# Recurrent gates as three passes of split operands in a hybrid decoder trunk

## The chip, the cores and the metric

The kernel runs on one core of one Trainium2 chip. The metric is the device time of one execution in microseconds, here the median of three runs. Engines are named as the profile names them: PE is TensorE (PEld its weight loads), DVE is VectorE, ACT is ScalarE, POOL is GpSimd, SP is SyncE, which issues the large transfers.

## The reference

A trunk of two layers on 256 tokens of width 2048. Each layer norms its input, projects it to all branches at once, runs three branches (a gated causal convolution, a recurrent block, sparse attention), weighs their outputs with sigmoid gates and projects the sum; a squared-ReLU MLP of width 8192 follows. The part that the change touches is the recurrent block (RG-LRU) on 768 channels, six blocks of 128:

```
def rg_lru(x, wa, ba, wx, bx, lam):
    xb = x.reshape(b, s, RNN_BLOCKS, RNN_BLOCK_W)
    r = sigmoid(einsum('bsnc,ncd->bsnd', xb, wa).reshape(b, s, d) + ba)
    i = sigmoid(einsum('bsnc,ncd->bsnd', xb, wx).reshape(b, s, d) + bx)
    log_a = -RG_C * softplus(-lam) * r
    a = exp(log_a)
    gated_x = sqrt(-expm1(2.0 * log_a)) * (i * x)
    _, h = associative_scan(_lin_combine, (a, gated_x), axis=1)
...
    r = causal_depthwise_conv(r_x, rnn_conv_w[l], rnn_conv_b[l])
    r = rg_lru(r, ...)
    p_b = (r * gelu(r_gate)) @ w_rnn_out[l]
```

All arrays are float32. `x` here is the block's convolved input, and `wa`, `wx` are six 128x128 matrices each, one per block and gate.

## The kernel before

Activations lie with channels on the 128 partitions and the 256 tokens (S) along the free dimension. All large matrices are streamed from HBM in tiles of up to 128x1024: SP fetches a tile `raw`, ACT copies it to `wh`, rounded to float32r (`wpart`, lines 192 to 196), and DVE subtracts to get the rest, `wl`. Activations are split in the same way by `split` (line 208) into two halves of one tile of the pool `hl` (34 tiles). A product of one 128x128 block (`tile2`, line 217) is then two instructions: `wh` times both halves (512 columns) and `wl` times the first half (256 columns), both in float32r. `wnext` keeps three weight tiles ahead (AHEAD), and the pool holds four.

The units of a layer follow the list PLAN (line 68): 38 units of the branches' inputs, then the 16 output-gate units "ga" with the 16 units "pa" of the convolution's output projection set between them from the seventh on, then "gb" with "pb" (recurrent branch), then "gc" with "pc" (attention), each in the same pattern, with the short units of the compression's matrices among "ga". A "pc" unit multiplies six blocks of `oh`, three per group of heads. A gate unit has 16 blocks. The layer ends with the output projection and the MLP.

Beside this stream run side tasks, as Python generators in the list `side`: `conv_task`, `rnn_task` and `attn_task`, strictly one after the other. Each step up to a `yield` is issued by `pump` (line 272) between weight tiles. `pump` works with a planner's clock per engine (`clk`): each helper (`tt`, `stt`, `ts`, `act`, `mm`, lines 132 to 157) adds a fixed charge for its instruction, what a side step charges on DVE and ACT counts 1.4 times (SLACK), and a step is issued only while the clocks of DVE and ACT are behind that of PE. So these charges decide where in the program a side task's steps stand. Ahead of the first unit that needs a task's result, `finish` (line 784) issues whatever steps are left of it.

From this program order a scheduler (line 1023) makes the order on each engine, by its own estimate of times; it may take a later instruction ahead where an earlier one's operands are not ready by that estimate. `keep` fixes the order of single instructions.

`rnn_task` (line 415) takes the six blocks `m` in turn: the two gates' matrices of the block come by a DMA that POOL issues (`ruw`, 128x256), the four-tap convolution makes `rc` on DVE, two plain float32 products (lines 423 and 424) make both gates in one PSUM tile, and Tanh, Exp and Sqrt on ACT, DVE arithmetic and a scan make the block's output, which is split into `rb_` tiles for "pb".

Of the kernel before, what the change touches and what calls it, by code (L numbers as in the profile page):

```python
# [10 lines left out]
F32R = mybir.dt.float32r  # L11
# [7 lines left out]
S = 256  # L19
# [74 lines left out]
def trunk(ctx: ExitStack, tc: tile.TileContext, a, out):  # L94
# [15 lines left out]
    def hl(dt=F32, name="hl"):  # L110
        return hlp.tile([128, 2, S], dt, tag="hl", name=name)

    def tmp(name="t"):
        return tp.tile([128, S], F32, tag="t", name=name)
# [4 lines left out]
    def big_ps():  # L119
        return psu.tile([128, 512], F32, tag="u", name="pu")  # L120

    def side_ps():
        return pss.tile([128, 512], F32, tag="s", name="pv")

    def fsz(ap):
        n = 1
        for s in ap.shape[1:]:
            n *= s
        return n


    def tt(o, x, y, op):
        clk["v"] += 0.07 + fsz(o) / 960
        return V.tensor_tensor(o, x, y, op=op)  # L134

    def stt(o, x, s, y, op0, op1):
        clk["v"] += 0.07 + fsz(o) / 960
        return V.scalar_tensor_tensor(o, x, s, y, op0=op0, op1=op1)  # L138

    def ts(o, x, s1, s2, op0, op1=None):  # L140
        clk["v"] += 0.07 + fsz(o) / 1920
        if op1 is None:
            return V.tensor_scalar(o, x, s1, None, op0=op0)
        return V.tensor_scalar(o, x, s1, s2, op0=op0, op1=op1)

    def act(o, x, f, bias=None, scale=1.0, accum=None):
        clk["act"] += 0.2 + fsz(o) / 1200
        kw = {}
        if bias is not None:
            kw["bias"] = bias  # L150
        if accum is not None:
            kw["accum_out"] = accum
        return A.activation(o, x, f, scale=scale, **kw)  # L153

    def mm(o, l, r, start, stop, passes=1):
        clk["pe"] += (passes * max(64, fsz(r)) if passes > 1 else max(256, fsz(r))) / 2400 + 0.002
        return T.matmul(o, l, r, start=start, stop=stop)  # L157

    def f32(ap):
        return ap.bitcast(F32)  # L160
# [47 lines left out]
    def split(dst, src, scale=None):  # L208

        if scale is None:  # L210
            act(dst[:, 0, :], src, AF.Copy)
            tt(dst[:, 1, :], src, f32(dst[:, 0, :]), ALU.subtract)
        else:
            act(dst[:, 0, :], src, AF.Copy, scale=scale)
            stt(dst[:, 1, :], src, scale, f32(dst[:, 0, :]), ALU.mult, ALU.subtract)
# [154 lines left out]
    def causal_conv(o, u, w, b, k):  # L370

        ts(o, u, w[:, k - 1:k], b, ALU.mult, ALU.add)
        yield
        for d in range(1, k):
            stt(o[:, d:], u[:, :S - d], w[:, k - 1 - d:k - d], o[:, d:], ALU.mult, ALU.add)
            yield
# [38 lines left out]
    def rnn_task(l, rx, gg, rb_out):  # L415
        rw = par[:, l, P_RW:P_RW + 24]
        for m in range(6):
            rc = tmp("rconv")
            ruw = tmp("ruw")
            keep(G.dma_start(ruw, a["rgw"][l, m]))  # L420
            yield from causal_conv(rc, rx[m], rw[:, 4 * m:4 * m + 4], par[:, l, P_RB + m:P_RB + m + 1], 4)
            p = side_ps()
            mm(p[:, :S], ruw[:, :128], rc, True, True, 4)
            mm(p[:, S:], ruw[:, 128:], rc, True, True, 4)
            tr, ti, t2 = tmp("tr"), tmp("ti"), tmp("t2")
            act(tr, p[:, :S], AF.Tanh, bias=hpar[:, l, 132 + m:133 + m], scale=0.5)
            act(ti, p[:, S:], AF.Tanh, bias=hpar[:, l, 138 + m:139 + m], scale=0.5)
            s2, s4 = sp2[:, l, m:m + 1], sp4[:, l, m:m + 1]

            act(t2, tr, AF.Tanh, bias=s2, scale=s2)  # L430
            act(tr, tr, AF.Exp, bias=s4, scale=s4)
            yield
            stt(t2, tr, 1.0, t2, ALU.add, ALU.mult)
            ts(tr, t2, -1.0, 1.0, ALU.mult, ALU.add)
            stt(t2, t2, 2.0, t2, ALU.subtract, ALU.mult)
            act(t2, t2, AF.Sqrt, scale=-0.25)
            yield
            stt(ti, ti, 1.0, rc, ALU.add, ALU.mult)
            tt(ti, ti, t2, ALU.mult)
            h = rc  # L440
            clk["v"] += 0.6
            V.tensor_tensor_scan(h, tr, ti, 0.0, op0=ALU.mult, op1=ALU.add)
            yield
            tt(h, h, gg[m], ALU.mult)
            r = hl(F32R, "rb_")
            split(r, h, 0.5)
            rb_out.append(r)
            yield
# [255 lines left out]
    for l in range(L):  # L704

        rc, rb = None, None
# [22 lines left out]
        def evict(nm, m, z):  # L729
# [16 lines left out]
            elif nm == "rgate":  # L746
# [5 lines left out]
                if m == 5:  # L752
                    rt = rnn_task(l, rx, gg, rbt)
                    side.append(rt)
# [26 lines left out]
        for ui, (nm, m) in enumerate(PLAN):  # L781
# [7 lines left out]
            if l == 0 and ui < 2:  # L789
                p = early[ui]  # L790
            else:
                p = big_ps()
# [22 lines left out]
        for m in range(KT):  # L815
            p = big_ps()
# [214 lines left out]
```

## Time and profile before

| | us |
|---|---|
| median of three runs | 2850.17 |
| lowest and highest | 2849.88 and 2850.19 |
| the profiled execution | 2849.82 |
| its span, first to last instruction | 2848.1 |

| engine | busy us | share of the span |
|---|---|---|
| PE | 2836.5 | 100% |
| PEld | 2490.8 | 87% |
| DVE | 2095.5 | 74% |
| ACT | 1473.7 | 52% |
| POOL | 91.1 | 3% |

A profile of one execution lists each instruction with its start and length from the span's start. A record's length includes the time in which the engine's pipeline drains, so consecutive records on PE overlap; what an instruction costs there is read from the distance of the starts. A group's line gives the count, then busy time and mean length, then the idle time before it and what ended that. PE's granted clock is full (0.999 on average).

### The profile page before, as it was taken

To read this page: it belongs to the slowest core of one execution; us is meant where nothing else is said; L and a number is where in the kernel's file an instruction comes from. 1 tells how busy PE (TensorE), PEld (TensorE's weight loads), DVE (VectorE), ACT (ScalarE), POOL (GpSimd) and SP (SyncE) were. 2 spreads that over 40 slices of the span, in tenths; PEclk is the share of its full clock that TensorE was granted. 3 is DMA by queue.
4 is the path that set the end of the run, shared out by engine and by line. 5 is a ranking of instruction groups with operands and counts; after the bars stand their busy time and mean duration, and the time that the engine had idled before them with its cause. 6 is when DMAs were issued, how large, how long until landed. Compare 5 with 4: busy or idle time off the path is not lost.

```text
span 2848.1 us, 43089 instructions
## 1 busy us (share of the span) xinstructions
PE 2836.5 (100%) x16420; PEld 2490.8 (87%) x16420; DVE 2095.5 (74%) x3388; ACT 1473.7 (52%) x2253; POOL 91.1 (3%) x88
## 2 busy tenths in 40 slices
PE   9999999999999999999999999999999999999998
PEld 7888888888888888888888888888888888888887
DVE  7988888777676676666779888786777766766655
ACT  6547765555444443443545587555554444434444
POOL 0000000002000000000200000000020000000001
PEclk9999999999999999999999999999999999999999
DMA  7555655465556555555555556545655555555554
GB/s 241 191 189 175 218 173 162 164 194 192 189 189 191 190 189 191 191 189 191 191 187 190 185 187 215 160 159 178 196 188 189 189 191 189 190 191 190 191 191 148
DMA packets 153454, 534.28 MB, mean 188 GB/s; under 512 B 17312, under 2 KB 18208, under 8 KB 153248
## 3 DMA queue, kind: packets, MB, share of 16 engines
q1 hardware_dynamic: 152192, 529.15, 56.6%
q8 instruction: 128, 2.10, 0.3%
q0 software_dynamic: 768, 2.13, 0.3%
q14 instruction: 78, 0.64, 0.1%
q10 hardware_dynamic: 288, 0.26, 0.0%
HBM read 529.37 MB, written 2.10 MB: 187 GB/s over the span
## 4 chain that ended last, share of the span: by engine, by line
PE 99%; DMA 0%; DVE 0%; ACT 0%; SPq 0%; issue 0%; POOLq 0%; DVEq 0%; ACTq 0%
PE pu L157 96%; PE pv L157 3%; PE pv L658 0%; DMA x<-in_xT_dram 0%; DMA raw<-in_win_dram 0%; DVE fin L134 0%; ACT wh L153 0%; PE pv L616 0%; DVE wl L134 0%; PE pv L526 0%; ACT xhl L153 0%; SPq L194 0%; SPq L688 0%; POOLq L1023 0%; DVE sq L134 0%
## 5 line engine op out<-in xcount | busy, mean ns | idle before, releaser
L153 ACT ACTIVATE wh<-raw 128x1024 fp32r<-128x1024 f32 (+2 forms) x1036 | 1067.9, 1031 | 1293.3 <-PE pu L157 682.1
L157 PE MATMUL pu<-xhl,wh 128*128 128x512 f32 x4800 | 1678.1, 393 | 0.9 <-DVE xhl L138 0.5
L134 DVE TENSOR_TENSOR wl<-raw,wh 128x1024 fp32r<-128x1024 f32 (+2 forms) x1036 | 1229.3, 1187 | 597.7 <-ACT wh L153 577.6
L157 PE MATMUL pu<-xhl,wl 128*128 128x256 f32 x4800 | 1346.3, 281 | 0.4 <-DVE wl L134 0.2
L157 PEld LDWEIGHTS pu<-xhl,wh 128*128 128x128 f32 x4800 | 898.2, 187 | 199.2 <-ACT wh L153 1.9
L157 PEld LDWEIGHTS pu<-xhl,wl 128*128 128x128 f32 x4800 | 906.8, 189 | 3.9 <-DVE wl L134 1.2
L157 PE MATMUL pu<-ah,wh 128*128 128x512 f32 x2016 | 699.1, 391 | 0.0
L157 PE MATMUL pu<-ah,wl 128*128 128x256 f32 x2016 | 564.5, 280 | 0.0
L157 PEld LDWEIGHTS pu<-ah,wh 128*128 128x128 f32 x2016 | 377.0, 187 | 82.7
L157 PEld LDWEIGHTS pu<-ah,wl 128*128 128x128 f32 x2016 | 381.0, 189 | 0.0
L134 DVE TENSOR_TENSOR x<-x,pu 128x256 f32<-128x256 f32 x316 | 132.8, 421 | 87.8 <-PE pu L157 82.6
L157 PE MATMUL pu<-yhl,wh 128*128 128x512 f32 x512 | 177.5, 393 | 0.0
L331 POOL TENSOR_TENSOR ssq<-ssq,sq 128x256 f32<-128x256 f32 x55 | 73.8, 1342 | 2175.3 <-ACT sq L153 2170.7
L157 PE MATMUL pu<-yhl,wl 128*128 128x256 f32 x512 | 141.7, 277 | 0.0
L157 PEld LDWEIGHTS pu<-yhl,wh 128*128 128x128 f32 x512 | 95.8, 187 | 22.0
L134 DVE TENSOR_TENSOR z<-pu,z 128x256 f32<-128x256 f32 x268 | 111.5, 417 | 0.8 <-ACT z L153 0.8
L138 DVE SCALAR_TENSOR_TENSOR cacc<-u,hpar,cacc 128x255 f32<-128x255 f32 (+14 forms) x240 | 103.5, 462 | 0.0
L153 ACT ACTIVATE z<-pu 128x256 f32<-128x256 f32 x268 | 98.2, 367 | 1.2 <-PE pu L157 1.2
L157 PEld LDWEIGHTS pu<-yhl,wl 128*128 128x128 f32 x512 | 96.2, 188 | 0.2
L157 PE MATMUL pu<-oh,wh 128*128 128x512 f32 x192 | 67.4, 391 | 0.0
L134 DVE TENSOR_TENSOR z<-z,rb 128x256 f32<-128x256 f32 x136 | 57.4, 424 | 4.3
L138 DVE SCALAR_TENSOR_TENSOR s<-z 128x256 f32<-128x256 f32 x128 | 54.1, 424 | 4.3
(295 smaller groups left out, 1702.7 us busy)
## 6 DMA issues: line engine op xcount, KB each, us to landing
raw<-in_win_dram SPq DMA_DIRECT2D x340, 512.0 KB, 3.3
raw<-in_wup_dram SPq DMA_DIRECT2D x256, 512.0 KB, 4.3
raw<-in_wdn_dram SPq DMA_DIRECT2D x256, 512.0 KB, 4.3
raw<-in_wo_dram SPq DMA_DIRECT2D x64, 512.0 KB, 3.3
raw<-in_wro_dram SPq DMA_DIRECT2D x32, 384.0 KB, 3.1
raw<-in_wao_dram SPq DMA_DIRECT2D x32, 384.0 KB, 3.1
raw<-in_wco_dram SPq DMA_DIRECT2D x32, 256.0 KB, 3.1
raw<-in_cw_dram SPq DMA_DIRECT2D x16, 512.0 KB, 4.6
```

What stands on the lines that cost most here:

```text
L134: return V.tensor_tensor(o, x, y, op=op)
L138: return V.scalar_tensor_tensor(o, x, s, y, op0=op0, op1=op1)
L153: return A.activation(o, x, f, scale=scale, **kw)
L157: return T.matmul(o, l, r, start=start, stop=stop)
L331: G.tensor_tensor(ssq[0], ssq[0], q, op=ALU.add)
```

## The change

In each of the six steps of `rnn_task`, the block's convolved input `rc` and its two matrices `ruw` are split into a float32r part and the rest, as the stream's operands are. Each gate is then three float32r products of 256 columns (first part by first part, first by rest, rest by first) that add up in the same PSUM half, where it was one plain float32 product. A `yield` stands between the splits and the products. The two new tiles come from the pool `hl`. In the planner's charges a block's products go from 2 x 4 x 256 to 6 x 256 columns, and two copies on ACT and two subtractions on DVE are added.

```diff
@@ rnn_task
             yield from causal_conv(rc, rx[m], rw[:, 4 * m:4 * m + 4], par[:, l, P_RB + m:P_RB + m + 1], 4)
+            rs, rws = hl(F32R, "rs"), hl(F32R, "rws")
+            split(rws, ruw)
+            split(rs, rc)
+            yield
             p = side_ps()
-            mm(p[:, :S], ruw[:, :128], rc, True, True, 4)
-            mm(p[:, S:], ruw[:, 128:], rc, True, True, 4)
+            for i in range(2):
+                o, (wh, wl) = p[:, i * S:(i + 1) * S], (rws[:, k, i * 128:(i + 1) * 128] for k in range(2))
+                mm(o, wh, rs[:, 0, :], True, False)
+                mm(o, wh, rs[:, 1, :], False, False)
+                mm(o, wl, rs[:, 0, :], False, True)
             tr, ti, t2 = tmp("tr"), tmp("ti"), tmp("t2")
```

## Rows read from the trace of the kernel before

**Rows 1.** The page: busy time by engine, and the chain that ended last.

```profile
PE 2836.5 (100%) x16420; PEld 2490.8 (87%) x16420; DVE 2095.5 (74%) x3388; ACT 1473.7 (52%) x2253; POOL 91.1 (3%) x88
...
PE 99%; DMA 0%; DVE 0%; ACT 0%; SPq 0%; issue 0%; POOLq 0%; DVEq 0%; ACTq 0%
```

**Rows 2.** Busy by stretch: length, PE, PEld, DVE, ACT, POOL; clock, DMA, GB/s.

```profile
216.00:332.00 116.00, 116.00 (x679) 101.98 (x678) 101.60 (x193) 93.24 (x155) 5.19 (x9) 1.00 0.60 197
...
1640.00:1726.00 86.00, 86.00 (x500) 75.68 (x499) 74.55 (x143) 70.12 (x114) 3.21 (x6) 1.00 0.59 195
```

**Rows 3.** Tile `ruw`: count, shortest/median/longest ns, first and last start in us.

```profile
L157 PE MATMUL pv<-rconv,ruw x48: 377/379/380, 232.9 to 1716.1; 128*128 128x256 f32 x48
```

**Rows 4.** Timeline of PE around the first block's gates: start, length in us.

```profile
232.55 0.39 PE L157 MATMUL pu<-xhl,wh 128*128 128x512 f32 x1
232.78 0.28 PE L157 MATMUL pu<-xhl,wl 128*128 128x256 f32 x1
232.90 1.03 PE L157 MATMUL pv<-rconv,ruw 128*128 128x256 f32 x4
233.57 0.58 PE L157 MATMUL pu<-xhl,wh 128*128 128x512 f32 x1
233.99 0.28 PE L157 MATMUL pu<-xhl,wl 128*128 128x256 f32 x1
```

**Rows 5.** Timeline of PE in the last unit (lines 886 to 888).

```profile
2828.42 0.40 PE L157 MATMUL pu<-wh,ah 128*128 128x256 f32 x2
2828.66 0.28 PE L157 MATMUL pu<-wl,ah 128*128 128x256 f32 x1
2828.78 0.40 PE L157 MATMUL pu<-wh,ah 128*128 128x256 f32 x2
```

**Rows 6.** Groups by line and tile: splits of 128x256 elsewhere in the kernel.

```profile
L153 ACT ACTIVATE ua<-lny 128x256 fp32r<-128x256 f32 x4 | 1.5, 406 | 0.0
L134 DVE TENSOR_TENSOR krl<-krf,krh x8: 416/418/421, 355.3 to 1762.1; 128x256 fp32r<-128x256 f32 x8
```

**Rows 7.** Timeline of DVE: one weight tile's subtraction.

```profile
283.37 1.21 DVE L134 TENSOR_TENSOR wl<-raw,wh 128x1024 fp32r<-128x1024 f32 x1
```

**Rows 8.** Timeline of PE: that tile's first use, and a later place.

```profile
285.44 0.28 PE L157 MATMUL pu<-xhl,wl 128*128 128x256 f32 x1
...
288.37 0.40 PE L157 MATMUL pu<-ua,wh 128*128 128x512 f32 x1
288.61 0.28 PE L157 MATMUL pu<-xhl,wl 128*128 128x256 f32 x1
```

**Rows 9.** The last block's output in layer 0: its reader and its writer.

```profile
L157 PE MATMUL pu<-rb__3455,wh x16: 391/396/473, 396.8 to 496.0; 128*128 128x512 f32 x16
...
L138 DVE SCALAR_TENSOR_TENSOR rb__3455<-rconv,rb__3455 x1: 419/419/419, 329.7 to 329.7; 128x256 fp32r<-128x256 f32 x1
```

**Rows 10.** Timeline of DVE: the last write of `oh` in either layer.

```profile
530.42 0.28 DVE L134 TENSOR_TENSOR oh<-pv,oh 128x128 fp32r<-128x128 f32 x1
...
1935.10 0.28 DVE L134 TENSOR_TENSOR oh<-pv,oh 128x128 fp32r<-128x128 f32 x1
```

**Rows 11.** Timeline of PE: the first product on `oh` in either layer.

```profile
541.92 0.39 PE L157 MATMUL pu<-oh,wh 128*128 128x512 f32 x1
...
1954.92 0.39 PE L157 MATMUL pu<-oh,wh 128*128 128x512 f32 x1
```

**Rows 12.** Timeline of ACT: the end of attention in layer 0.

```profile
508.29 0.46 ACT L153 ACTIVATE e<-pv,nm 128x256 f32<-128x256 f32 x1
...
515.20 1.23 ACT L153 ACTIVATE eh<-pv 128x384 fp32r<-128x384 f32 x3
...
522.09 0.49 ACT L153 ACTIVATE eh<-pv 128x384 fp32r<-128x384 f32 x1 [0.42 <-PE pv L658]
```

**Rows 13.** Busy by stretch, as rows 2: two "pc" units, then a gate unit.

```profile
541.93:546.25 4.32, 4.32 (x27) 3.83 (x26) 3.07 (x5) 2.85 (x6) 0.00 (x0) 1.00 0.57 185
546.09:551.80 5.71, 5.71 (x35) 5.05 (x34) 4.99 (x10) 2.94 (x6) 0.00 (x0) 1.00 0.73 215
```

## The prediction

> **What bounds the kernel now.** The page's first two parts and its chain of waits come first: TensorE (PE) is busy for 2836.5 of 2848.1 us, and 99% of the chain that ended last is PE, nearly all of it products of the weight stream at line 157 [rows 1]. The table by stretch shows the same where the gates run: in 216 to 332 us (layer 0) and 1640 to 1726 us (layer 1) PE is busy all the time, VectorE (DVE) for 101.60 of 116.00 and 74.55 of 86.00 us, ScalarE (ACT) for 93.24 and 70.12 [rows 2]. So a PE microsecond saved is a microsecond of the end, and work on ACT or DVE costs nothing until PE waits for it. Two things can make it wait: a weight tile that is split too late, and an activation that is ready too late. In the order of PE's instructions, I look at the gates, then at the tightest weight tile, then at the next place where PE needs what the side tasks make: the first product on `oh`, at unit "pc" 0.
>
> **What the change removes on PE.** The gates are 24 plain float32 products, 48 records, the first at 232.9 and the last at 1716.1 us [rows 3]. The PE timeline of the first channel: four records start at 232.90, the next stream product at 233.57, and that one takes 0.42 us to its successor (233.99) where an ordinary 512-column product takes 0.23 (232.55 to 232.78) [rows 4]. The channel therefore costs 233.99 - 232.90 - 0.23 = 0.86 us. The eleven others follow the same pattern. 12 x 0.86 = 10.3 us.
>
> **What it adds on PE.** Six float32r products of 128x128 by 256 columns per channel. The same form runs in the kernel's tail: from 2828.42 to 2828.78 us three start, 0.12 us each, and so on through the unit [rows 5]. Six are 0.72 us, and the slowed product behind the float32 ones goes. Per channel 0.86 - 0.72 = 0.14 us, in all 12 x 0.14 = 1.7 us. Bounds: half of an ordinary 512-column product, 0.23 / 2 = 0.115 us, would give 0.69 a channel and 2.0 in all; if the slowed product (0.42 - 0.23 = 0.19 us too long) stayed behind the new ones too, the channel would lose 0.05 and all together 0.6 us. I take 1.7, since the tail's rows have the very shape and the same three passes.
>
> The Trainium skill (FP8 and Floating Point Precision, section TensorE Precision Notes) says that true FP32 makes four passes through the array. By passes alone three in place of four would save a quarter, 12 x 0.215 = 2.6 us, against 1.7 by the rows. The trace has 0.43 us a float32 product against 0.12 for one pass, 3.6 times, so a narrow pass costs more than its share and I go by the rows.
>
> **What it adds beside PE.** Two splits per channel: on ACT two copies of 128x256 to float32r at 0.41 us, on DVE two subtractions at 0.42 us [rows 6]; 0.82 and 0.84 us a channel, 9.8 and 10.1 us in all. In layer 0's stretch 4.9 us more on ACT and 5.0 on DVE would still fit (DVE 106.6 of 116). Work that hides them: the weight stream on PE. What is queued behind them on ACT and DVE are the splits of weight tiles `wh` and `wl`, for which PE waits in the end. The tightest such tile: its subtraction starts at 283.37 and takes 1.21 us, so it ends at 284.58 [rows 7], and PE uses it at 285.44 [rows 8], a margin of 0.86 us. Worked out for each tile in the same manner, this margin is around 6 us in most of the stream; it falls to 1 to 4 in 265 to 340 and 1680 to 1770 us, where the short "pa" tiles come. One split set in front of a tile there could cost PE up to 0.84 + 0.82 - 0.86 = 0.8 us.
>
> DMAs, queues on SP and POOL, and PSUM tiles stay as they are. `ruw` is free earlier (after its split, no longer after the product). Two more tiles of the pool `hl` live for a short time per channel; by a count of what lives then (gates, values, `ua`, `rb`) some 30 of 34 are in use: no wait taken, and a short one is in the range.
>
> **What it moves.** This is the larger matter. The side tasks run one after the other (convolution, recurrent branch, attention), and `pump` (lines 272 to 279) lets a step run only when the planner's clocks of DVE and ACT are behind that of PE. By lines 132 to 157 a channel charges DVE: the convolution 0.20 + 3 x 0.33, then 0.34 + 0.20 + 0.34, then 0.34 + 0.34 + 0.60, then 0.34 + 0.34, about 4.0; the two new subtractions add 2 x 0.34 = 0.67, a sixth more. All of it counts 1.4 times (SLACK). A gate unit charges PE 16 x 0.324 = 5.18 and DVE 2 x 1.14 + 2 x 0.34 = 2.95, so it leaves 2.23 for side steps; 0.94 more per channel then needs 0.94 / 2.23 = 0.42 of a unit, 2.2 of the planner's us, 13 for six channels. During "pa" units nearly nothing is left for side steps, and each added step waits for a whole call of `pump`; carried through the plan unit by unit, the charges put the recurrent task's end 25 (layer 0) and 31 (layer 1) planner's us later (these are places in the program, not times on the chip). Its result has room: in layer 0 the last channel's is written at 329.7 and PE first takes it at 396.8 us [rows 9], and layer 1 has more. Attention starts that much later, and it has less room. By the same arithmetic its last step stood 18 and 31 planner's us ahead of "pc" 0; now it comes right at it in layer 1, and in layer 0 some steps are left over, which `finish` (line 784) places in front of "pc" 0.
>
> The trace says what that is worth. Now `oh` is complete at 530.42 + 0.28 = 530.7 and 1935.4 us [rows 10] and PE begins "pc" 0 at 541.92 and 1954.92 [rows 11]: 11.2 and 19.5 us of slack. One block of a unit takes PE 0.35 us (232.55 to 232.90 [rows 4]) where the planner charges 0.324, so a planner's us is 1.08 us: the last step is placed 19.5 and 33.6 us ahead of "pc" 0, and its result lags its place by 8.3 and 14.1 us. The chain shows why: from the last softmax exponentials at 508.29 over the four transposed groups (515.20, 522.09) to the last `oh` at 530.7 are 22 us of ACT, DVE and PE in turn [rows 12]. With the last step placed at "pc" 0, `oh` is complete some 8 to 14 us after PE arrives there. No row shows PE waiting there, so I bound it. Below: nothing, if other work fills the gap. The order is not rigid: at 288.37 one product of the next unit (`ua`) stands inside a unit on `xhl` [rows 8], so the scheduler fills PE with later work when the next is not ready. What can fill: the first half of "pc" 0 and 1, whose three blocks of `oh` are done earlier (half of their 4.32 us, 2.2), the next gate unit (5.71 us [rows 13]), the first halves of "pc" 2 and 3 (2.2), and attention's own last products: about 10 us. Above: 8.3 + 14.1 = 22 us, if nothing fills. Against 10 us of cover, 8 to 14 us leave 0 in layer 0 and up to 4 in layer 1, somewhat more if the left-over steps crowd. I take 2.5 us for both together, nearer to zero since rows 8 show the filling.
>
> **The sum.** The profiled execution took 2849.82 us, 1.7 of it outside its span; the median shown is 2850.17, 0.35 above. From the median: 2850.17 - 1.7 + 2.5 = 2851.0.
>
> **The rivals.** (1) The end of attention becomes the bound: the gap in front of "pc" 0 is not filled. For it: the lag of 8 to 14 us is measured, and layer 0's left-over steps come in one piece. Against: the filling at 288.37. It decides slower once the two stalls exceed 1.7 + 5.7 = 7.4 us. Price: half filled, 11 us, 2859.5; not filled, 22 us, 2870.5. (2) Weight tiles come late: for it the margin of 0.86 us; against, that the planner spreads the side steps when they cost more, so that DVE is no denser than now. Nine or ten tiles 0.8 us late make 7.5 us, 2856; fewer stay within the bound of no change. (3) Everything is filled and only the gates tell: 2848.5. It is the lower part of my forecast. (4) Faster than that: the gates' 10.3 us bound any gain, and six products can't be had for nothing (2.0 us by the bound above); over 0.2% would need stalls elsewhere to vanish, and the page has PE busy all along.
>
> **Chances.** A difference of 0.2% (5.7 us) is about what a measurement of this kernel can tell from no change. Stalls of 0 to 7.4 us (2848.5 to 2855.9, rival 3 within): 0.71. Rival 1: 0.21, rival 2: 0.06, together slower 0.27. Faster: 0.02. The range from 2848.0 to 2862 takes in the bounds of the gates' price and rival 1 with half its gap filled; what lies above, with little filled, is about 0.1.
>
> **What would show it.** Right: PE's busy time in the gates falls to 0.72 us a channel with starts of 0.12; the recurrent task's last channel comes some 25 to 35 us later than now (1716.1 in layer 1); the last `oh` is written within a few us of the first product on `oh`, and products on `xhl` stand between the halves of "pc" 0. Wrong: idle time of PE put down to `oh`, in front of the fourth block of "pc" 0, of over 4 us a layer (rival 1); idle time put down to `wl` in 265 to 370 or 1680 to 1800 us (rival 2); attention that ends where it does now, in which case the moved steps were mis-sized.

## The result, and the profile after

The changed kernel takes 2876.3 us (median of four executions; 2873.28 to 2877.46) against 2850.2 before: ratio 1.0089, 95% interval 1.0078 to 1.0101, so 26 us slower. The forecast was 2851.0, the range ended at 2862. The profiled execution took 2873.28 us, its span 2871.5 (2848.1 before).

The page of the changed kernel: busy time by engine, and the chain that ended last (the lines of [rows 1]).

```profile
PE 2844.7 (99%) x16444; PEld 2494.7 (87%) x16444; DVE 2099.5 (73%) x3412; ACT 1484.9 (52%) x2277; POOL 91.4 (3%) x88
...
PE 97%; DVE 1%; ACT 1%; DMA 1%; issue 0%; SPq 0%; POOLq 0%; DVEq 0%; ACTq 0%
```

PE's busy time rose by 8 us though its products became cheaper, the chain has 1% each of DVE and ACT in it where it had none, and the splits are there (24 records more on ACT and DVE each). Where PE waited, in the view of waits (us in total, times, longest):

```profile
PE pu L157 <- DVE z L134: 11.8, 7, 3.1
...
PE pu L157 <- DVE oh L134: 1.4, 2, 0.7
PE pu L157 <- ACT wh L153: 1.1, 2, 0.8
...
PE pu L157 <- DVE wl L134: 0.6, 3, 0.2
PE pv L157 <- DVE rs L134: 0.5, 1, 0.5
```

The largest line is new: in the kernel before, PE never waits for `z`. The tile `z` takes the low half of a finished unit out of PSUM (ACT), DVE adds the high half, and only then is the unit's PSUM bank free. A product that waits for `z` waits for one of four banks. Weight tiles (`wh` 1.1 and `wl` 0.6 us, against 0.4 and 0.2 before) matter little.

The stretches (length, PE, PEld, DVE, ACT, POOL; clock, DMA, GB/s) in which this happens, the first and third as in [rows 2], the other two at the attention's ends; below them the kernel before at its attention's ends:

```profile
216.00:332.00 116.00, 112.16 (x653) 98.38 (x652) 94.90 (x180) 86.91 (x150) 5.19 (x9) 0.97 0.57 187
540.00:570.00 30.00, 26.75 (x138) 22.14 (x137) 20.91 (x48) 16.27 (x41) 0.00 (x0) 0.94 0.34 107
1640.00:1726.00 86.00, 83.53 (x491) 73.42 (x490) 70.93 (x136) 66.45 (x115) 2.15 (x4) 1.00 0.52 174
1968.00:1992.00 24.00, 21.26 (x121) 17.72 (x120) 13.79 (x30) 11.93 (x25) 0.00 (x0) 1.00 0.35 114
```

```profile
540.00:570.00 30.00, 30.00 (x175) 26.43 (x174) 22.80 (x38) 17.09 (x30) 0.00 (x0) 1.00 0.58 186
1952.00:1976.00 24.00, 24.00 (x140) 21.14 (x139) 18.17 (x31) 14.12 (x24) 0.00 (x0) 1.00 0.60 185
```

PE stands for 3.8, 3.3, 2.5 and 2.7 us in them; before it was busy all the time. DVE and ACT are less busy in the gate stretches than before (94.90 against 101.60, 86.91 against 93.24 in layer 0), although the splits are added: part of the side steps now stands behind the stretch (the recurrent branch's last result comes at 368.6 us, before at 330.1), so it is not their time that runs short here.

The gate stretch of layer 0, the ACT timeline of the changed kernel (start, length; in brackets the idle time before and who ended it):

```profile
270.02 1.06 ACT L153 ACTIVATE wh<-raw 128x1024 fp32r<-128x1024 f32 x1 [0.46 <-ACT t L153]
271.24 0.42 ACT L153 ACTIVATE rb__2703<-rconv 128x256 fp32r<-128x256 f32 x1 [0.15 <-DVE rconv L134]
271.56 0.40 ACT L153 ACTIVATE rws<-ruw 128x256 fp32r<-128x256 f32 x1
271.87 0.40 ACT L153 ACTIVATE rs<-rconv 128x256 fp32r<-128x256 f32 x1
272.80 1.06 ACT L153 ACTIVATE wh<-raw 128x1024 fp32r<-128x1024 f32 x1 [0.53 <-ACT rs L153]
273.87 1.28 ACT L153 ACT_TABLE_LOAD   x1
275.17 0.47 ACT L153 ACTIVATE tr<-pv,hpar 128x256 f32<-128x256 f32 x1
275.54 0.47 ACT L153 ACTIVATE ti<-pv,hpar 128x256 f32<-128x256 f32 x1
275.89 0.60 ACT L153 ACTIVATE t<-tr,sp 128x256 f32<-128x256 f32 x1
276.39 1.20 ACT L153 ACTIVATE z<-pu 128x256 f32<-128x256 f32 x4
```

and PE beside it:

```profile
264.23 0.28 PE L157 MATMUL pu<-xhl,wl 128*128 128x256 f32 x1
264.34 0.39 PE L157 MATMUL pu<-ua,wh 128*128 128x512 f32 x1
...
272.55 0.28 PE L157 MATMUL pu<-xhl,wl 128*128 128x256 f32 x1
...
273.40 0.86 PE L157 MATMUL pv<-rs,rws 128*128 128x256 f32 x5 [0.46 <-DVE rs L134]
277.37 0.77 PE L157 MATMUL pu<-ua,wh 128*128 128x512 f32 x1 [3.11 <-DVE z L134]
```

Four evictions stand one behind the other at 276.39; their units had ended between 264.3 us, where the first gives way to a unit on `ua`, and 272.7. PE finishes the gate products at 274.3, finds all four banks taken and begins again at 277.37, 3.1 us later. A part of that is ACT's own: its table load ends at 275.15, 0.9 us behind the gate products, and `tr` stands behind it. Layer 1 has the same pattern once, and a third pause stands in front of "pb" 0, where no gate product is near:

```profile
1697.09 0.47 PE L157 MATMUL pu<-xhl,wh 128*128 128x512 f32 x1 [2.47 <-DVE z L134]
...
1865.19 0.47 PE L157 MATMUL pu<-rb__16498,wh 128*128 128x512 f32 x1 [1.73 <-DVE z L134]
```

What follows the pause of layer 0 on PE's clock, by stretch, and in the last line the place of 1865.19:

```profile
270.00:275.00 5.00, 3.80 (x23) 3.04 (x21) 4.39 (x8) 4.28 (x6) 0.55 (x1) 1.00 0.80 288
275.00:282.60 7.60, 5.23 (x17) 4.49 (x18) 6.69 (x18) 4.81 (x12) 0.00 (x0) 0.55 0.21 71
282.60:290.00 7.40, 7.40 (x44) 6.42 (x44) 5.06 (x11) 5.56 (x9) 0.00 (x0) 1.00 0.49 142
...
1860.00:1872.00 12.00, 10.27 (x55) 8.68 (x54) 9.16 (x27) 4.96 (x14) 0.00 (x0) 0.86 0.37 116
```

The granted clock is 0.55 of full from 275.0 to 282.6, that is mostly the lower level of 1.2 GHz, with full speed on either side. It fell around the pause. The 540 to 570 row (0.94) has a second such place, the row of 1860 to 1872 (0.86) the third.

At the end of attention in layer 0, ACT and then PE, with the like place of layer 1 last:

```profile
561.58 1.06 ACT L153 ACTIVATE wh<-raw 128x1024 fp32r<-128x1024 f32 x1 [1.77 <-PE pu L157]
562.55 0.36 ACT L153 ACTIVATE z<-pu 128x256 f32<-128x256 f32 x1
```

```profile
541.41 0.40 PE L157 MATMUL pu<-oh,wh 128*128 128x512 f32 x1
...
558.92 0.50 PE L157 MATMUL pu<-oh,wh 128*128 128x512 f32 x1 [0.69 <-DVE oh L134]
...
564.29 0.51 PE L157 MATMUL pu<-oh,wh 128*128 128x512 f32 x1 [1.92 <-DVE z L134]
...
1990.07 0.50 PE L157 MATMUL pu<-oh,wh 128*128 128x512 f32 x1 [1.92 <-DVE z L134]
```

The last `oh` is written by DVE at

```profile
559.85 0.29 DVE L134 TENSOR_TENSOR oh<-pv,oh 128x128 fp32r<-128x128 f32 x1 [0.34 <-ACT oh L153]
...
1985.63 0.29 DVE L134 TENSOR_TENSOR oh<-pv,oh 128x128 fp32r<-128x128 f32 x1 [0.34 <-ACT oh L153]
```

that is at 560.1 and 1985.9 us, 18.7 and 14.7 us behind PE's first product on `oh` (541.41 and 1971.27), where before it was 11.2 and 19.5 us ahead [rows 10, 11]. Units "pc" 0, 1 and 2, of which the first halves are done, and the gate unit between them hold the four banks for that long. When `oh` is there, ACT's next instruction is a weight tile's split that itself waits for PE, the eviction `z` stands behind it, and PE waits for `z`.

To sum it up I take, for each product on PE, the time from its start to the next start, and subtract the median of this for products of its shape, the same median in both kernels. The products at their medians come to 2823.9 us before and 2822.1 after: -1.8. What lies above the medians at full clock is 16.4 us before and 36.2 after, in half-clock stretches 0 and 5.4. In all -1.8 + 19.8 + 5.4 = 23.4 us, the difference of the spans. Of the excess after, 7.1 us lie in 200 to 300 us, 5.6 in 1600 to 1800, 9.6 in 500 to 600 and 7.7 in 1900 to 2000, where the kernel before has 0.4, 1.0, 1.4 and 1.3: 11.3 us more at the gates and 14.6 at the two ends of attention. The other windows nearly cancel, though not for want of a stall: 1800 to 1900 us holds the third pause and its slow stretch.

### The profile page after: what moved, and what is told of

It is laid out like the page before. It is cut to its first block, busy times and chain, and to the rows that moved or that the text cites. A ratio compares the mean times of both kernels' runs of the same rounds, so it can differ in the third digit from the quotient of the medians.

```text
span 2871.5 us, 43190 instructions
## 1 busy us (share of the span) xinstructions
PE 2844.7 (99%) x16444; PEld 2494.7 (87%) x16444; DVE 2099.5 (73%) x3412; ACT 1484.9 (52%) x2277; POOL 91.4 (3%) x88
## 4 chain that ended last, share of the span: by engine, by line
PE 97%; DVE 1%; ACT 1%; DMA 1%; issue 0%; SPq 0%; POOLq 0%; DVEq 0%; ACTq 0%
PE pu L157 94%; PE pv L157 2%; ACT wh L153 0%; DVE wl L134 0%; PE pv L665 0%; DMA x<-in_xT_dram 0%; DMA raw<-in_win_dram 0%; DMA raw<-in_cw_dram 0%; DVE fin L134 0%; DVE z L134 0%; PE pv L623 0%; PE pv L533 0%; DVE el L134 0%; ACT eh L153 0%; ACT L153 0%
```

## The experiments

Medians in us; the kernel before, run again beside each group of them, took 2849.6 to 2849.7.

| the kernel with | as it is | own buffers for `z` |
|---|---|---|
| before | 2849.7 | 2851.4 |
| before, three more gate units ahead of "pc" | 2849.7 | |
| before, new charges and pause only | 2866.0 | |
| the same, three more gate units ahead of "pc" | 2861.8 | |
| after, plain products | 2866.4 | 2862.0 |
| after | 2876.3 | 2863.9 |
| after, old charges, no pause | 2879.1 | 2860.6 |
| after, attention's charges x1.2 | 2872.0 | 2857.1 |
| after, three more gate units | 2870.3 | 2852.4 |
| after, three more gate units and x1.2 | | 2851.8 |
| after, five banks for the units | 2878.5 | |

**Old charges.** Theory: the change moves the side pieces in the program, and that is the whole loss. (Of each change the lines that matter are shown; ... stands for the others.)

```
+ was = dict(clk)
  split(rws, ruw)
  split(rs, rc)
- yield
  ...
+ clk.update(was, pe=was["pe"] + 2 * (4 * S / 2400 + 0.002))
```

> All instructions of the changed kernel (splits and three-pass products), but the planner's three clocks are charged for a channel as before the change and the extra pause between splits and products is gone, so the side pieces are handed out where they were before. Theory P (placement: the higher charges and the pause move side pieces, evictions z come late on ScalarE, PSUM banks fill, TensorE waits): 2848 to 2853 us. Theory L (the added ScalarE and VectorE work of some 1.7 us a channel, wherever it stands): 2868 to 2876 us. Theory C (the gate products wait for the splits): 2858 to 2872 us, since the pause that gave the splits time is gone.

2879.1 us, ratio 1.0099 (1.0082 to 1.0116): over all three expectations, and the theory of placement alone falls. Attention does end in time again (last `oh` 544.8, first product on it 556.0; the excess in 500 to 600 us is 2.0). But without the pause the products stand right behind their splits, and PE waits for the splits and again for `z`:

```profile
274.15 1.95 PE L157 MATMUL pv<-rs,rws 128*128 128x256 f32 x6 [3.77 <-ACT rs L153]
278.34 0.77 PE L157 MATMUL pu<-xhl,wh 128*128 128x512 f32 x1 [2.24 <-DVE z L134]
```

**Charges alone.** The other way round: no split, no new product, only the planner's bookkeeping and the pause. Against the kernel before:

```
+ clk["v"] += 2 * (0.07 + S / 960)
+ clk["act"] += 2 * (0.2 + S / 1200)
+ yield
+ pe0 = clk["pe"]
  ...
+ clk["pe"] = pe0 + 6 * (S / 2400 + 0.002)
```

> The kernel before with plain float32 gate products and no splits; only the planner is charged as if splits and six products were there, and the extra pause stands in the task. Theory P: 2870 to 2880 us (the gates 1.7 us longer than in the changed kernel, its stalls all there). Theories L and C: 2848 to 2853 us, as before the change.

2866.0, ratio 1.0056 (1.0041 to 1.0071). A kernel that does what the kernel before does is 16 us slower because its side pieces stand elsewhere. It is not the 2870 to 2880 of theory P either: against the changed kernel with the gates' 1.7 us put back some 12 us are missing, and the view by stretch says which.

```profile
540.00:560.00 20.00, 16.75 (x88) 13.45 (x87) 12.58 (x32) 11.20 (x30) 0.00 (x0) 0.96 0.21 71
...
216.00:332.00 116.00, 116.00 (x680) 102.02 (x679) 98.08 (x182) 89.97 (x149) 5.19 (x9) 1.00 0.58 196
```

The gate stretch is full; the attention's end is not (3.25 us idle in 20). PE's waits for `z` at the attention's ends and in front of "pb" 0 are in this kernel too, 5.6 us in three waits.

**Splits made, not read.** The two plain products stand in place of the six; splits, charges and pause stay.

```
- for i in range(2):
  ...
+ mm(p[:, :S], ruw[:, :128], rc, True, True, 4)
+ mm(p[:, S:], ruw[:, 128:], rc, True, True, 4)
+ clk["pe"] = pe0 + 6 * (S / 2400 + 0.002)
```

> The changed kernel with its splits, charges and pause, but the gate products are the two plain float32 ones on the unsplit matrix and tokens; the split tiles are made and not read. Theories P and L: 2875 to 2880 us (the products 1.7 us longer in all, everything else as it is). Theory C: 2850 to 2862 us, since no product waits for a split.

2866.4, ratio 1.0055 (1.0040 to 1.0070), the same as charges alone and in none of the expected ranges. So the splits' 0.8 us on ACT and on DVE a channel cost nothing, and theory L falls. The other 10 us come when the products read the splits. Theory C had the place right and the size of the direct wait wrong: in the changed kernel PE waits 0.5 us for `rs`, and 3.1 and 2.5 us for `z` behind it.

**Five banks.**

```
- psu = ...(name="psu", bufs=4, ...)
- pss = ...(name="pss", bufs=4, ...)
+ psu = ...(name="psu", bufs=5, ...)
+ pss = ...(name="pss", bufs=3, ...)
```

> The changed kernel with five PSUM banks for the main stream's units and three for the side work, in place of four and four. If TensorE waits because finished units hold their banks while their eviction z stands late on ScalarE (part of theory P), a fifth bank bears one unit's delay of 6.9 us more: 2855 to 2868 us. If banks do not matter (L or C): 2873 to 2880 us; if three side banks hold the side work up: over 2880 us.

2878.5, ratio 1.0099 (1.0084 to 1.0114): no help. PE waits 3.83 us for `z` at 278.12. With three side banks the order moved as well, so this run decides little.

Then I looked at the order of ACT's instructions by the number in which the program allocates their tiles. `z`, `tr`, `ti`, `t` and others share one pool of twelve. In the changed kernel the first writes of this pool's tiles stand on ACT in strict order of allocation: the four `z` at 276.39 were allocated behind `tr`, `ti` and `t`, and these wait for the gate products, which wait for the splits. These numbers are in the program and not in the views shown here, so the theory needs a run of its own. Theory R: the shared pool makes the evictions wait.

**Own buffers for `z`.**

```
- tp = ...(name="tp", bufs=12)
+ tp = ...(name="tp", bufs=9)
  ...
- z = tmp("z")
+ z = tp.tile([128, S], F32, tag="z", name="z", bufs=4)
```

> The changed kernel with one thing more: the tile z that takes a finished unit out of PSUM has four buffers of its own, and the pool of temporaries it came from keeps nine of its twelve. Theory R (z is handed its buffer in the order of the program, behind tr, ti and t2 of the gates and behind the attention's temporaries; when these wait for the splits, the evictions of up to four units stand behind them and PSUM fills): the big waits for z go, 2848 to 2856 us. Theory A (the stalls at the attention's end are the late hand-out of side pieces, whatever the buffers): the gates recover 10 us, the attention's 12 to 16 us stay, 2860 to 2868 us. Theory C (TensorE waits for the splits themselves): 2868 to 2876 us.

2863.9, ratio 1.0047 (1.0034 to 1.0059): 12.4 us come back, and 14 stay, which is what theory A said; theory R's 2848 to 2856 is missed, since the buffers do not cure the attention's ends. Own buffers for `z` end the gate stalls:

```profile
268.01 0.37 ACT L153 ACTIVATE z<-pu 128x256 f32<-128x256 f32 x1
...
270.54 0.36 ACT L153 ACTIVATE z<-pu 128x256 f32<-128x256 f32 x1
...
271.32 0.37 ACT L153 ACTIVATE z<-pu 128x256 f32<-128x256 f32 x1
...
274.23 0.40 ACT L153 ACTIVATE rws<-ruw 128x256 fp32r<-128x256 f32 x1
274.54 0.40 ACT L153 ACTIVATE rs<-rconv 128x256 fp32r<-128x256 f32 x1
```

```profile
268.00:280.00 12.00, 12.00 (x71) 10.46 (x70) 10.35 (x19) 10.69 (x20) 0.55 (x1) 1.00 0.62 204
```

Three evictions now run ahead of the splits, PE is busy throughout, and its clock stays full. In the view of waits `z` falls from 11.8 us to

```profile
PE pu L157 <- DVE z L134: 3.8, 2, 1.9
```

which are the two attention ends; the pause in front of "pb" 0 is gone too. None of the span's excess lies at half clock any more, where 5.4 us did.

**The same buffers without the change.**

> The kernel before with the same own buffers for z (four, and nine for the other temporaries). It shows what the buffers bring without the change: its evictions of z come at most 7.9 us late and no bank is waited for, so all theories say 2847 to 2852 us. If it falls to 2845 us or less, the buffers help anyway and what they bring in the changed kernel is no cure of the change.

2851.4, ratio 1.0006 (0.9998 to 1.0015): no gain, so the buffers cure something that the change brought.

**Attention handed out earlier.**

```
+ slack = 1.2 if side[0].__name__ == "attn_task" else SLACK
  ...
- clk["v"] += (clk["v"] - v0) * (SLACK - 1)
+ clk["v"] += (clk["v"] - v0) * (slack - 1)
  ...
```

> The changed kernel, but the planner stretches the attention task's charges by 1.2 in place of 1.4, so that the attention is handed out earlier and ends before the third projection. Theory A: the 6.7 and 6.4 us at the two attention ends and their share of the slow clock go, the gate stretches stay: 2856 to 2863 us. Theory R: the same order of the buffers still holds z back in the gate stretches and wherever the attention's pieces now stand; at least the 10 us of the gates stay, 2858 to 2872 us. If it falls under 2855 us both are wrong.

2872.0, ratio 1.0081 (1.0067 to 1.0095): 4 us of the 14 or so that theory A wanted, and just within theory R's range. In layer 1 the last `oh` comes at 1978.9 us, 7 us earlier and 4.2 behind PE's first product on it, and PE's waits there are gone. In layer 0 it comes at 559.8 all the same, still 13.6 us behind, and PE waits as before; why it comes no earlier was not traced. And a wait of 1.7 us for `z` is new, at 441.81.

**Own buffers, old charges.**

> The changed kernel's instructions with the planner's charges of before and no pause (the run that took 2879 us), and own buffers for z. Theory R: the banks no longer fill, what is left is TensorE's own wait for the splits in front of some gate products (4.0, 1.3 and 1.3 us seen in that run at products that follow the splits at once): 2850 to 2862 us. Theory C: these waits are the loss and stay, 2868 us or more.

2860.6, ratio 1.0040 (1.0028 to 1.0053), as theory R said, though not for its reason. Attention ends in time, PE waits 0.2 us for `rs`; what it waits for now is weight tiles, 4.7 us more than in the kernel before. Of the 11 us that are lost this is not all; the rest was not traced.

```profile
PE pu L157 <- DVE wl L134: 3.9, 7, 1.0
...
PE pu L157 <- ACT wh L153: 1.4, 2, 0.9
```

So the charges are no mere bookkeeping: where they do not spread the added splits, the prediction's second rival appears.

**A later third projection.** Its cover is made larger by three gate units.

```
- k = 0
+ k, d = 0, 9 if n == "c" else DEFER
  ...
- while m >= DEFER and k * (KT - DEFER) < (m + 1 - DEFER) * KT:
+ while m >= d and k * (KT - d) < (m + 1 - d) * KT:
```

> The changed kernel, but the third branch's projections begin after nine of its gate units instead of six, so the attention has three units of 5.55 us more before its output is wanted. Theory A (about 15 us of the loss is the attention's end meeting the third projection, whose banks stay full while its last halves are made): both attention ends fall back to the 1.3 us of excess that they have in the kernel before, the gate stretches keep their 10 us: 2856 to 2863 us. If the attention's late pieces only take the stall along (they are late by their own chain, not by the plan): 2868 to 2876 us.

> The changed kernel with both: own buffers for z, and three more gate units before the third projection. If the loss is these two and nothing else: 2847 to 2853 us, level with the kernel before. If something else of the change costs (the added work on ScalarE and VectorE): 2855 us or more.

> The kernel before with three more gate units before the third projection. Its attention ends in time anyhow (1.3 us of excess at each end), so this brings nothing: 2848 to 2852 us. If it falls to 2846 us or less the later start helps by itself and cures nothing of the change.

Alone it gives 2870.3, ratio 1.0074 (1.0061 to 1.0086), within its second expectation: in layer 0 attention's late pieces take the stall along, and the last `oh` comes at 572.9 us, 12.8 later than in the changed kernel; with own buffers 2852.4, ratio 1.0011 (1.0002 to 1.0020); in the kernel before 2849.7, ratio 1.0001 (0.9992 to 1.0010). With both, PE is busy through the place where it stood for 3.3 us:

```profile
540.00:570.00 30.00, 30.00 (x176) 26.33 (x175) 18.27 (x35) 15.62 (x31) 0.00 (x0) 1.00 0.39 128
```

and none of its waits is for `z` or `oh` any more. So late evictions and the attention's late end are, to 3 us, the whole loss, and neither remedy helps the kernel before. The two are not independent: with own buffers as well the last `oh` comes at 561.6 us, 11 earlier than with the later start alone. Alone, the later start still leaves PE a wait for `z`:

```profile
578.98 0.50 PE L157 MATMUL pu<-oh,wh 128*128 128x512 f32 x1 [1.43 <-DVE z L134]
```

> The changed kernel with own buffers for z and the attention's charges stretched by 1.2 instead of 1.4. The first brought 12 us and the second 4 us, one by one. If the second works on the attention's end alone they add up: 2857 to 2861 us; if z's buffers had held the earlier attention pieces up as well, more comes back: 2849 to 2856 us.

2857.1, ratio 1.0026 (1.0016 to 1.0036): the two add up to a little more than the sum of 12.4 and 4.3.

**What was left.**

> The changed kernel with own buffers for z, and its gate products the two plain float32 ones that do not read the splits (which are made and not read). If the gate stretches stalled because products that wait for splits hold tr, ti and t2, and behind these the evictions z, then own buffers bring nothing more once the products do not wait: 2863 to 2868 us, as the plain products without own buffers (2866.4). If the buffers cure something else too: 2852 to 2858 us.

> The kernel before with only the planner's charges and the pause of the change (2866 us by itself), and three more gate units before the third projection. If the 16 us are the two attention ends: 2849 to 2854 us. If the moved order costs elsewhere too: 2856 us or more.

> The changed kernel with own buffers for z, three more gate units before the third projection, and the attention's charges stretched by 1.2. In the version with the first two the trace still shows some 5 us of excess at the attention's ends over the kernel before. If the earlier hand-out takes it away: 2847 to 2850 us, level with the kernel before or up to 1.8 us under it; if not, 2851 to 2854 us.

Plain products with own buffers take 2862.0, ratio 1.0043 (1.0031 to 1.0056), 4 us below those without and just under the first expectation, so the buffers cure something besides products that wait for splits: without them PE waits 1.73 us for `z` in front of "pb" 0 in this kernel too and runs at half clock behind it, with them it does not. With own buffers, products that read the splits cost 1.9 us more than plain ones (2863.9 against 2862.0); with the shared pool 9.9 (2876.3 against 2866.4). It takes both for the gate stalls. Charges alone with the later projection take 2861.8, ratio 1.0044 (1.0030 to 1.0058): only 4 of the 16 us return, so the expectation that a later start cures the moved order by itself was wrong; PE still waits 3.6 us for `z` and 1.7 for `wh` in this kernel (1.1 of the latter at the kernel's start). All three remedies give 2851.8, ratio 1.0009 (1.0000 to 1.0017), no better than two. No version here beats the kernel before. Whether the gates' 1.8 us could be kept stays open: the cured kernels have some 4 us more of small gaps in PE's starts than the kernel before, spread over the gate stretches and the attention's ends, which I did not trace further.

## Why the prediction was wrong

- **What bounds the kernel: right.** PE's waits and the half clock that followed some of them are the whole loss.
- **The gates on PE: right.** -1.8 us by the start intervals, against -1.7. The timeline has the 0.12 us of the tail's rows [rows 5]:

```profile
238.55 0.28 PE L157 MATMUL pv<-rs,rws 128*128 128x256 f32 x1
238.67 0.28 PE L157 MATMUL pu<-xhl,wl 128*128 128x256 f32 x1
```

- **The added splits beside PE: right by size, wrong by what hangs on them.** They lengthened nothing by themselves (2866.4 with, 2866.0 without), and weight tiles stayed in time but for one wait of 0.8 us, the size that the prediction gave a late tile. The step that failed is the sentence that what is queued behind the splits on ACT and DVE are the splits of weight tiles. What mattered were the evictions `z`, which stand behind whatever waits for the splits; the prediction's "PSUM tiles stay as they are" gave the banks no price. The view that would have told was the order of ACT's instructions by pool: the prediction counted the pool `hl` and did not look at the pool of temporaries that `tr`, `ti`, `t` and `z` share. This term was zero; it is 11.3 us by the windows and 12.4 by the run with own buffers, half clock included.
- **The move of attention: right in direction and place, too short.** The last channel's products came at 1763.8 us (1716.1 before), the recurrent branch's last result in layer 0 at 368.6 (330.1 before): 47.7 and 38.5 us later, where 25 to 35 had been said. Counted by its products, the weight stream was then 9.5 and 0.3 us behind the kernel before, so the side steps moved by some 38 us against it in both layers. Attention's end met "pc" 0 in both layers, with products on `xhl` between the halves of "pc" 0.
- **The price of that: mis-sized.** `oh` was 18.7 and 14.7 us late for 8 to 14 reckoned; the steps left over in layer 0 come in one piece, which the prediction named and priced at "somewhat more". The cover was there but ended: from 541.4 to 558.9 us PE did the first halves of "pc" 0 to 2, a gate unit and attention's own products, 13.9 us of work by the medians, and lost 3.6; the like place in layer 1 lost 2.3. Then all four banks were held, and PE stood for `z`, 1.9 us in either layer, and lost 1.5 more at half clock in layer 0. The rest is small gaps, most of them ahead of "pc" 0. The term was 2.5 us; the excess at the two ends rose by 9.6 - 1.4 and 7.7 - 1.3, in all 14.6 us. That is the first rival, between its 11 and its 22 us. Its sign was to be a wait for `oh` of over 4 us a layer; the wait for `oh` is 0.7 a layer, and the rest goes under other names, `z` first. With attention's charges x1.2 an `oh` 4.2 us late (layer 1) cost no wait and one 13.6 us late (layer 0) did, so some cover is real and 18.7 us are beyond it.
- **The sum.** 2851.0 - 2.5 + 14.6 + 11.3 = 2874.4, against 2873.28 profiled and 2876.3 in the median; the pause in front of "pb" 0 is in neither term and is offset by smaller gaps elsewhere. With the first rival alone the forecast would still have been 2863, above the range; its chance, 0.21, leaned on a cover of 10 us that no row had shown filled.

The Trainium skill (PSUM — Partial Sum Buffer, section Engine vs sequencer instructions) says that ScalarE's queue is strictly first in, first out. The trace agrees with it: units that had ended up to 12 us earlier were evicted only at 276.39, behind `tr`, `ti` and `t`.

## What to carry to other kernels

An added operation for which PE itself waits 0.5 us can cost 12 us (here) if a shared buffer pool puts the evictions of PSUM behind whoever waits for it; before costing it, list which tiles share a pool with its readers, and give the evictions their own. A cover of other work counts only if it has somewhere to put its result: look at what holds the banks, not only at how many products could run. And in a kernel whose order comes from a planner's charges, a change of the charges is a change of the program, to be priced like one (here 16 us for new charges and a pause, with no instruction changed).

## What the runs showed of the hardware

A pause of PE of 3.1 us was followed by a stretch of which most ran at the lower clock (0.55 of full from 275.0 to 282.6 us), so that the pause cost more than its length: 5.4 us in all over three such places. It is not the length of the pause alone: 1.92 us of idle time at the attention's end in layer 0 (564.29) went with a lower clock (0.94 in 540 to 570), the same wait in layer 1 did not (1.00 in 1968 to 1992), nor did it with own buffers for `z`. And 1.73 us at 1865.19 went with one (0.86 in 1860 to 1872), 2.47 us at 1697.09 did not (1.00 in 1640 to 1726).
